# Decayed cumulative sum behind a matmul: four of 32 groups by seven block products, in an order laid out by a planner

## The chip, the cores and the metric

The kernel runs on one core of a Trainium2 chip. The metric is the device time in microseconds of one execution. Engines: PE (matmuls; PEld is its weight load), DVE (vector), ACT (scalar), POOL (GpSimd), SP (here it only issues stores). Every engine works through its own instruction list in order; waits on other engines are semaphores written into the program when it is built.

## What is computed

```python
# x (16, 2048, 1024), w (1024, 1024), decay (1024), all float32
xw = x @ w
out[:, 0, :] = xw[:, 0, :]
for t in range(1, S):
    out[:, t, :] = decay[None, :] * out[:, t - 1, :] + xw[:, t, :]
```

A matmul of 32,768 rows by 1024 x 1024, then a first-order recurrence along time for each batch and column.

## The kernel before

**Tiling.** Time is cut into chunks of 512 (`TL`), four to a batch, 64 in all; two chunks make a group (`groups`), 32 groups. The last group runs as two single chunks. The 1024 output columns are eight blocks of 128 (`n`). One step is one group times one column block: 264 steps, `slots`. A step's result lies with its 128 columns on the partitions and its 1024 times along the free dimension, as the recurrence wants it.

**A chunk's way in.** `load` (L105) brings a quarter of a chunk by a DMA issued from POOL, float32 in memory to bf16 on the chip, 256 KB as landed (four such per chunk, ring `xb` of three). `turn` (L115) transposes it in 32 x 32 blocks on DVE into `xw`; `part` (L123) has ACT copy it, in two halves ("X", "Y"), into `xt` (ring of five), the form that PE reads.

**A step.** `matmul` (L131): eight slices k of the inner dimension times two chunks, 16 matmuls of 128 x 128 by 512 columns, into `ps`, two PSUM banks; there are three such tiles. Then the recurrence, in one of two ways:

- *full* (`run`, L228; every fourth step): DVE scans all 1024 times out of PSUM into `so`, one instruction.
- *paired* (three of four steps): ACT copies the result to `xs` (L185) and writes the decayed even times to `h` (L170); POOL adds them to the odd times (L205); DVE scans the odd times alone with the squared decay (L210), 512 elements; ACT decays the scanned odd times (L170 again), and POOL adds the even ones (L253, "fill").

`save` (L257) and `zero` (L201, L199) carry the last value from one group of a batch to the next. `back` (L265) has DVE transpose `so` in 32 x 32 blocks into `ot`. Four steps fill one `ot` tile, here called a lump, 2 MB; when its fourth back transpose is recorded, `Outlet.store` (L289) issues four DMAs of 512 KB from SP. `ot` is a ring of four, `so` of four, `xs` of three, `h` of four.

**Order.** Everything is pinned to the order in which the Python program records it. The first 34 steps and the last 20 follow `agenda`, a table written by hand (P: paired beginning, S: scan, C: even times, B: back, T: turn, X/Y: chunk copies, L: a load; small letters are single instructions). The steps between follow `usual` with `later`: step s issues the paired beginning of s, the scan of s-1, the fill of s-1, the back transposes of s-2, and one load, with a chunk's turn and copies a fixed number of steps ahead. Line 395 on is the ending, where PE transposes the last tiles and ACT and DVE copy them out (L399).

Of the kernel before, what the change touches and what calls it, by code (L numbers as in the profile page):

```python
# [2 lines left out]

# [6 lines left out]
FP32 = mybir.dt.float32  # L10
# [15 lines left out]
def kernel(  # L26
# [26 lines left out]
    nc = tc.nc  # L53
# [12 lines left out]
    R = K // 2  # L66
    CH = D // 2
    CR = CH // NQ

    const = ctx.enter_context(tc.tile_pool(name="const", bufs=1))  # L70
    sb = ctx.enter_context(tc.tile_pool(name="sb", bufs=1))
# [20 lines left out]
    wcols = wsb.rearrange("p k (h r) q i -> p k h q r i", h=2)  # L92

    def ot_tile(nj):
        return ring(sb, "ot", 4, [128, nj, CR])

    xb_of = {}
    xw_of = {}
# [19 lines left out]

    def part(c, copy, m0, m1, j0=0, j1=NJ):
        if c not in xt_of:  # L120
            xt_of[c] = ring(sb, "xt", 5, [128, M, 2, TL], BF16)
        src = xw_of[c][:, m0:m1, j0:j1].rearrange("p m j i e -> p m e (j i)")
        pin(copy(out=xt_of[c][:, m0:m1, :, j0 * P:j1 * P], in_=src))  # L123

# [16 lines left out]
    class Tile:  # L141
# [3 lines left out]
        def __init__(self, g, n, ps, outlets):  # L145
            self.b, self.t0 = chunks[g[0]]
            self.T = TL * len(g)
            self.n, self.ps, self.outlets = n, ps, outlets
            self.paired = n % R != R - 1
            if len(tiles) in flips or len(tiles) - len(slots) in flips:  # L150
                self.paired = not self.paired
            self.turn = len(tiles)
            self.lot = sum(t.paired for t in tiles)
            self.prev = None if self.t0 == 0 else last[n]
            if self.t0 + self.T < S:
                last[n] = const.tile([128, 1], FP32, name=f"keep{n}", bufs=2)
                self.keep = last[n]
            else:
                self.keep = None

        @property
        def so(self):
            if not hasattr(self, "held"):
                self.held = sb.tile([128, 2 * TL + 2], FP32, name=f"so{self.turn % 4}")
            return self.held

        def decayed(self, src, h=None):
            if h is None:
                h = ring(sb, "h", 4, [128, TL])[:, 0:self.T // 2]
            pin(nc.scalar.activation(  # L170
                out=h, in_=src, func=mybir.ActivationFunctionType.Copy,
                scale=dec[:, self.n:self.n + 1]))
            return h
# [5 lines left out]
                self.zero()  # L179
                self.join()  # L180

        def copy(self):
            self.xs = sb.tile([128, 2 * TL], FP32, name=f"xs{self.lot % 3}")[:, 0:self.T]
            for t, ps in self.parts():
                pin(nc.scalar.copy(out=self.xs[:, t:t + ps.shape[1]], in_=ps))  # L185

        def odd(self):
            self.g = ring(sb, "h", 4, [128, TL])[:, 0:self.T // 2]
            for t, ps in self.parts():
                size = ps.shape[1]  # L190
                self.decayed(ps[:, 0:size:2], self.g[:, t // 2:(t + size) // 2])

        def parts(self):
            some = self.ps if isinstance(self.ps, tuple) else (self.ps,)
            return [(i * self.T // len(some), ps) for i, ps in enumerate(some)]

        def zero(self):
            if self.prev is None:
                pin(nc.gpsimd.memset(self.so[:, 1:2], 0.0))  # L199
            else:  # L200
                pin(nc.scalar.copy(out=self.so[:, 1:2], in_=self.prev))  # L201

        def join(self):
            odds = self.xs[:, 1:self.T:2]
            pin(nc.gpsimd.tensor_tensor(out=odds, in0=self.g, in1=odds, op=ALU.add))  # L205

        def scan(self):
            T, n, so = self.T, self.n, self.so
            if self.paired:
                pin(nc.vector.tensor_tensor_scan(  # L210
                    out=so[:, 3:T + 2:2],
                    data0=squares[-1][:, n:n + 1].to_broadcast([128, T // 2]),
                    data1=self.xs[:, 1:T:2],
                    initial=0.0 if self.prev is None else self.prev,
                    op0=ALU.mult,
                    op1=ALU.add,
                ))
            else:
                for t, ps in self.parts():
                    self.run(ps, t, ps.shape[1])  # L220

        def run(self, ps, t, size):
            n, so = self.n, self.so
            if t:
                before = so[:, t + 1:t + 2]
            else:
                before = 0.0 if self.prev is None else self.prev
            pin(nc.vector.tensor_tensor_scan(  # L228
                out=so[:, t + 2:t + 2 + size],
                data0=dec[:, n:n + 1].to_broadcast([128, size]),  # L230
                data1=ps,
                initial=before,
                op0=ALU.mult,
                op1=ALU.add,
            ))
# [5 lines left out]
        def complete(self):  # L241
            if self.paired:
                self.even()
                self.fill()
            if self.keep is not None:
                self.save()

        def even(self):
            self.h = self.decayed(self.so[:, 1:self.T + 1:2])

        def fill(self):
            T = self.T
            pin(nc.gpsimd.tensor_tensor(  # L253
                out=self.so[:, 2:T + 2:2], in0=self.h, in1=self.xs[:, 0:T:2], op=ALU.add))

        def save(self):
            pin(nc.scalar.copy(out=self.keep, in_=self.so[:, self.T + 1:self.T + 2]))  # L257

        def back(self, half=None):
# [13 lines left out]
    class Outlet:  # L273


        def __init__(self, ns, nj, half=0, queues=(nc.sync,), pieces=1):
            self.pieces = pieces
            self.ns, self.missing, self.half = ns, set(ns), half
            self.nj, self.t0, self.queues = nj, half * nj * P, queues
            self.ot = ot_tile(nj)  # L280

        def store(self, b, t0):
            n0 = self.ns[0]
# [132 lines left out]
    def turn_and_load(c):  # L416
# [58 lines left out]
        18: "g16 T7 L h15 j16 p17 g17 B14 z17 c15 X7",  # L475
        19: "S16 j17 p18 B15 L g18 L S17 k16 h16 z18 j18",
        20: "Y7 S19 L c16 k17 h17 T8 k19 L c17",
        21: "p20 g20 L S18 X8 j20 B17 B19",
        22: "L h18 p21 c18 B16 k18 g21 B18 Y8 z20 L j21 S20",
        23: "p22 z21 z22 S21 L h20 g22 T9 c20 h21",  # L480
        24: "k21 k20 j22 S23 X9 L c21 Y9 B20 L",
        25: "B23 k23 p24 B21 g24 z24 j24 S22 z25",
        26: "p25 T10 k22 h22 g25 c22 S24 X10 j25",
        27: "B22 p26 S25 g26 z26 Y10 j26",
        28: "S27 h25 h24 c25 S26 c24",
        29: "B27 h26 c26 T11 p28 g28 j28 B24",
        30: "p29 B25 g29 z28 j29 S28 z29 S29",
        31: "h28 p30 c28 B26 g30 h29 B28 j30 z30",
        32: "c29 S31 S30 h30 B29 c30 p32 g32 z32 j32 B30 B31 L L",
        33: "p33 g33 z33 j33 S32 h32 c32 k32 L L",  # L490
        -20: "z-20",
        -19: "p-20 g-20",
        -18: "j-20 S-19 S-20 k-19 B-19",
# [16 lines left out]
        -1: "S-2 h-4 c-4 a-1 b-1 V",  # L510
    }
    flips = (1, 13, 15, -19, -18, -11, -8, -6, -3, -2)
    later = {}
    begun = {"T": 12, "X": 11, "Y": 11}
    for c in range(5, nch):
        first = c // 2 * K
        ahead = (7, 6, 4) if c % 2 else (11, 10, 8)
        for letter, a in zip("TXY", ahead):
            if c >= begun[letter]:
                later.setdefault(first - a, []).append(f"{letter}{c}")  # L520

    def usual(s):
        paired = [t.paired for t in tiles]
        do = [f"P{s}"] if paired[s] else []
        if paired[s - 1]:
            do.append(f"S{s - 1}")
        if not paired[s]:
            do.append(f"S{s}")
        do.append(f"C{s - 1}")
        if paired[s - 2]:  # L530
            do.append(f"B{s - 2}")
        if not paired[s - 1]:
            do.append(f"B{s - 1}")
        return do + later.get(s, []) + ["L"] * (2 if len(loads) > NQ else 1)

    def rest(s):
        do = [f"S{s - 1}"] if tiles[s - 1].paired else []
        do.append(f"C{s - 1}")
        if tiles[s - 2].paired:
            do.append(f"B{s - 2}")  # L540
        return do + [f"B{s - 1}"] + later.get(s, []) + ["L"] * len(loads)

    def perform(do):
        for deed in do:
            deeds[deed[0]](int(deed[1:] or 0))

    perform(agenda[-99].split())
    spares = [spare] + [ring(psp, "spare1", 1, [128, TL])]
    for step, (g, n) in enumerate(slots):
        T = TL * len(g)  # L550
        left = step - len(slots)
        if n % R == 0:
            ns, nj = range(n, n + R), T // P
            outlets = [Outlet(ns, nj)]
        if left == -R:
            outlets = []
        if step == 0:
# [48 lines left out]
            for k, l in todo:  # L606
                matmul(ps[:, l * TL:(l + 1) * TL], n, k, xt_of[g[l]])
        tiles.append(Tile(g, n, ps, outlets))
        do = agenda.get(step, agenda.get(left) if left >= -20 else None)
        if do is None:  # L610
            do = usual(step)
        else:
            do = do.split()
            if left == -20:
                do = rest(step) + do
        perform(do)
    assert not loads
# [1 line left out]
_INS = ['x', 'w', 'decay']  # L619
# [26 lines left out]
```

## Time and profile before

| | |
|---|---|
| median of 3 runs | 904.89 us (904.84 to 904.93) |
| the profiled execution, its own time | 905.68 us |
| its span | 903.9 us |
| granted TensorE clock, mean | 0.999 |
| matmuls, weight loads | 4217, 4217 |
| DMA | 204.77 MB moved, mean 227 GB/s |
| HBM read, written | 138.42 MB, 134.22 MB |

One execution is profiled. Busy time is the time in which an engine works on an instruction; an instruction's duration overlaps the start of the next by some 0.1 us, so the distance from start to start says more of what a full engine can do. A stretch is a piece of the span, in us from its start. "L131" is a line of the kernel above.

### The profile page before, as it was taken

Reading aid. Unit: us, or ns where it says so; the run is one execution under the profiler, and the core shown is the slowest. Engines: PE = TensorE matmul, PEld = TensorE weight load, DVE = VectorE, ACT = ScalarE, POOL = GpSimd, SP = SyncE. Lnnn points to the kernel's source line nnn. Section 1 sums busy time; section 2 is a strip of 40 time slices with the busy share of each in tenths; the row PEclk is TensorE's granted clock in tenths of the full one; section 3 lists DMA queues with packets and bytes.
Section 4 is the critical chain, followed back from the end, with each engine's and each line's share of the span. In section 5 each row is a group of like instructions: output and inputs, shape, how many; then the busy total and the mean of one; then the engine's idle time right before and its main releaser. Section 6 shows DMA issues by size and latency. Waiting matters only on the chain.

```text
span 903.9 us, 12113 instructions
## 1 busy us (share of the span) xinstructions
PE 896.4 (99%) x4217; PEld 412.7 (46%) x4217; DVE 825.5 (91%) x628; ACT 686.3 (76%) x957; POOL 656.7 (73%) x755
## 2 busy tenths in 40 slices
PE   8999999999999999999999999999999999999997
PEld 5544444444444444444444444444444444444444
DVE  4999998999999999999998999999999999999997
ACT  4899967777877877877778778778777787787742
POOL 7978678777767768677677677777777776776632
PEclk9999999999999999999999999999999999999999
DMA  9999999999999999999999999999999999999868
GB/s 186 190 215 215 226 256 217 215 237 236 254 242 260 243 251 257 248 237 226 224 237 229 224 229 229 230 224 229 231 227 228 233 232 222 226 233 211 176 143 235
DMA packets 402542, 204.77 MB, mean 227 GB/s; under 512 B 8752, under 2 KB 401456, under 8 KB 402480
## 3 DMA queue, kind: packets, MB, share of 16 engines
q1 hardware_dynamic: 265168, 134.76, 61.0%
q0 software_dynamic: 137024, 68.70, 56.6%
q8 instruction: 33, 0.54, 0.2%
q10 hardware_dynamic: 288, 0.52, 0.2%
q14 instruction: 29, 0.24, 0.1%
HBM read 138.42 MB, written 134.22 MB: 302 GB/s over the span
## 4 chain that ended last, share of the span: by engine, by line
PE 97%; DMA 1%; POOL 0%; issue 0%; DVE 0%; DVEq 0%; POOLq 0%
PE ps L131 96%; DMA xb<-in_x_dram 1%; PE spare L131 1%; POOL xb L105 0%; PE spare L395 0%; PE ps L395 0%; DVE h L399 0%; DVE xw L115 0%; DVEq L115 0%; POOLq L630 0%
## 5 line engine op out<-in xcount | busy, mean ns | idle before, releaser
L131 PE MATMUL ps<-xt,wsb 128*128 128x512 bf16 (+1 forms) x4028 | 866.3, 378 | 0.0
L131 PEld LDWEIGHTS <-wsb 128*128 128x128 bf16 x4168 | 407.5, 98 | 478.0 <-ACT wsb L313 0.8
L205 POOL TENSOR_TENSOR xs<-h,xs 128x512 f32<-128x512 f32 (+1 forms) x190 | 242.8, 1278 | 188.1 <-ACT h L170 85.3
L185 ACT COPY xs<-ps 128x1024 f32<-128x1024 f32 (+1 forms) x190 | 188.9, 994 | 152.9 <-PE ps L131 148.1
L265 DVE STREAM_TRANSPOSE ot<-so 128x1024 f32<-128x1024 f32 (+1 forms) x260 | 300.0, 1191 | 2.1 <-POOL so L199 1.1
L253 POOL TENSOR_TENSOR so<-h,xs 128x512 f32<-128x512 f32 (+1 forms) x190 | 241.0, 1270 | 43.7 <-ACT h L170 27.8
L123 ACT COPY xt<-xw 128x2048 bf16<-128x2048 bf16 (+3 forms) x136 | 242.3, 1790 | 8.7 <-DVE xw L115 8.7
L105 POOL DMA_DIRECT2D xb<-in_x_dram x264 | 174.0, 660 | 5.6 <-DMA xb<-in_x_dram 3.2
L170 ACT ACTIVATE h<-so,dec 128x512 f32<-128x512 f32 (+1 forms) x190 | 145.3, 766 | 28.7 <-DVE so L210 25.2
L115 DVE STREAM_TRANSPOSE xw<-xb 128x2048 f32<-128x2048 f32 (+3 forms) x78 | 147.4, 1901 | 8.0 <-DMA xb<-in_x_dram 7.9
L210 DVE TENSOR_TENSOR_SCAN so<-spare,keep,xs 128x512 f32<-128x512 f32 (+1 forms) x97 | 119.9, 1239 | 26.7 <-POOL xs L205 26.4
L210 DVE TENSOR_TENSOR_SCAN so<-spare,xs 128x512 f32<-128x512 f32 x93 | 113.3, 1219 | 27.4 <-POOL xs L205 24.5
L170 ACT ACTIVATE h<-ps,dec 128x512 f32<-128x512 f32 (+1 forms) x190 | 130.0, 684 | 0.0
L228 DVE TENSOR_TENSOR_SCAN so<-dec,ps 128x1024 f32<-128x1024 f32 x34 | 76.8, 2260 | 1.0 <-ACT h L170 1.0
L228 DVE TENSOR_TENSOR_SCAN so<-dec,keep,ps 128x1024 f32<-128x1024 f32 (+1 forms) x35 | 75.9, 2168 | 0.2 <-issue 0.2
L257 ACT COPY keep<-so 128x1 f32<-128x1 f32 x136 | 25.3, 188 | 9.5 <-DVE so L228 9.0
L201 ACT COPY so<-keep 128x1 f32<-128x1 f32 x97 | 18.4, 191 | 2.7 <-DVE ot L265 2.4
L131 PE MATMUL spare<-xt,wsb 128*128 128x512 bf16 (+3 forms) x60 | 12.6, 329 | 0.0
L131 PE MATMUL ps<-xw,wsb 128*128 128x256 bf16 (+3 forms) x68 | 11.2, 301 | 0.4 <-DVE xw L115 0.4
L199 POOL MEMSET so<- 128x1 f32 x93 | 10.7, 117 | 0.6 <-DVE ot L265 0.6
L331 PE MATMUL spare<-idle 128*128 128x512 bf16 x22 | 6.8, 479 | 1.2 <-DVE idle L321 1.2
L306 POOL DMA_DIRECT2D ot<-in_w_dram x12 | 6.6, 552 | 1.7 <-DMA xb<-in_x_dram 0.8
(39 smaller groups left out, 37.9 us busy)
## 6 DMA issues: line engine op xcount, KB each, us to landing
out_dram<-ot SPq DMA_DIRECT2D x248, 512.0 KB, 10.9
xb<-in_x_dram POOLq DMA_DIRECT2D x248, 256.0 KB, 7.9
out_dram<-ot SPq DMA_DIRECT2D x12, 256.0 KB, 4.2
ot<-in_w_dram POOLq DMA_DIRECT2D x12, 128.0 KB, 5.6
xb<-in_x_dram POOLq DMA_DIRECT2D x8, 128.0 KB, 5.4
out_dram<-xb SPq DMA_DIRECT2D x3, 256.0 KB
xb<-in_x_dram POOLq DMA_DIRECT2D x4, 144.0 KB, 7.0
ot<-in_w_dram ACTq DMA_DIRECT2D x2, 256.0 KB, 5.2
```

The lines of the kernel that those rows point to most:

```text
L105: pin(nc.gpsimd.dma_start(out=xb_of[c][quad(q), j0:j1], in_=_ap(x, [[D, P], [P * D, j1 - j0], [1, CQ]], (b * S + t0 + j0 * P) * D + q * CQ)))
L115: pin(nc.vector.transpose(out=dst.rearrange("p (m j i) -> p j m i", m=M, i=P)[:, j0:j1, m0:m1], in_=src.rearrange("p (j m c) -> p j m c", ...
L123: pin(copy(out=xt_of[c][:, m0:m1, :, j0 * P:j1 * P], in_=src))
L131: pin(nc.tensor.matmul(out=ps[:, t0:t1] if ps.shape[1] >= t1 else ps, lhsT=lhs, rhs=rhs, start=(k == 0 and t0 == start), stop=(stop and k ...
L170: pin(nc.scalar.activation(out=h, in_=src, func=mybir.ActivationFunctionType.Copy, scale=dec[:, self.n:self.n + 1]))
L185: pin(nc.scalar.copy(out=self.xs[:, t:t + ps.shape[1]], in_=ps))
L205: pin(nc.gpsimd.tensor_tensor(out=odds, in0=self.g, in1=odds, op=ALU.add))
L210: pin(nc.vector.tensor_tensor_scan(out=so[:, 3:T + 2:2], data0=squares[-1][:, n:n + 1].to_broadcast([128, T // 2]), data1=self.xs[:, 1:T:2 ...
L228: pin(nc.vector.tensor_tensor_scan(out=so[:, t + 2:t + 2 + size], data0=dec[:, n:n + 1].to_broadcast([128, size]), data1=ps, initial=befor ...
L253: pin(nc.gpsimd.tensor_tensor(out=self.so[:, 2:T + 2:2], in0=self.h, in1=self.xs[:, 0:T:2], op=ALU.add))
L257: pin(nc.scalar.copy(out=self.keep, in_=self.so[:, self.T + 1:self.T + 2]))
L265: pin(nc.vector.transpose(out=outlet.ot[:, :, c0:c0 + P], in_=self.so[:, 2 + t0:2 + t0 + nj * P].rearrange("p (i t) -> p i t", t=P)))
```

## The change

A *merged* group is worked out by seven products of blocks instead of eight. The group's 1024 input columns are cut in two halves of 512 (k below and above 4) and the chunks and column blocks in pairs: two chunks a, b times two column blocks n0, n1, each a sum over two halves, are eight products of four matmuls. Sums of the inputs (`sums`, three on DVE, one on POOL, once a group) and differences of the weights (`differ`, on POOL, 20 in all, made once ahead of the first merged group, kept in `wd`) allow seven. Their results are put together through PSUM: a product is accumulated, copied out by ACT (`lift`), further products are accumulated on top, copied or joined again (`join`, DVE, an addition or subtraction of a PSUM operand and an SBUF one, 512 elements). For two column blocks: four copies and three joins. Steps of merged groups are all paired and take their recurrence from `so`, since no whole result stands in PSUM.

Groups 10, 15, 20 and 25 are merged. In the groups around them fewer steps are full: of groups 4 to 30 (steps 34 to 243) 36 steps are, by `SHARE`.

Steps 34 to 243 are no longer recorded by `usual` but by `steady`: every instruction becomes a `Job` with an engine, a cost, a key (a due time) and what it comes after; `in_order` lays them out, engine by engine, always the ready job with the lowest key, and records them in that order. Rings change: `ot` 3 (was 4), `xt` 4 (was 5), `so` 7 (was 4), `xs` is gone (the paired steps work in place in `so`). A turn is recorded in two halves. Loads get evenly spaced due times, at least 2.8 apart, 50 ahead of their group (74 ahead of a merged one). A lump is stored by sixteen DMAs of 128 KB, everywhere. The hand-written steps 21 to 33 move X8 to X10 and drop the last loads, which the planner takes over.

```diff
+    OTS, XTS, SOS, HS = 3, 4, 7, 4
+    FROM, TO = 34, 244
+    SUMS, SUMT = ('dve', 'dve', 'dve', 'pool'), -16
+    WBY, WLEAD, WSTEP = "pool", 130, 6
+    SHARE = {-1: 0.25, 0: 0, 1: 0.08, 2: 0.16, 3: 0.25, 9: 0.25}
+    merged = (10, 15, 20, 25)
...
-        return ring(sb, "ot", 4, [128, nj, CR])
+        return ring(sb, "ot", OTS, [128, nj, CR])
...
-        def __init__(self, ns, nj, half=0, queues=(nc.sync,), pieces=1):
+        def __init__(self, ns, nj, half=0, queues=(nc.sync,), pieces=4):
...
-        24: "k21 k20 j22 S23 X9 L c21 Y9 B20 L",
+        24: "X8 k21 k20 j22 S23 Y8 L c21 B20 L",
...
-        32: "c29 S31 S30 h30 B29 c30 p32 g32 z32 j32 B30 B31 L L",
-        33: "p33 g33 z33 j33 S32 h32 c32 k32 L L",
+        32: "c29 X10 Y10 S31 S30 h30 B29 c30 p32 g32 z32 j32 B30 B31",
+        33: "p33 g33 z33 j33",
...
+    GAP = 0.19
+    BEGUN = {"pe": 0.0, "act": 7.6, "dve": 8.3, "pool": 9.0}
+    LAND = 11.0
+    STORED = 13.0
+    PASS = 0.2158
+    cost = {"p": .91, "g": .6, "z": .12, "j": 1.27, "S": 1.16, "D": 2.2, "h": .68, "c": 1.27,
+            "k": .11, "B": 1.14, "T": 1.14, "X": 1.79, "L": .66, "half": .5, "both": .62,
+            "sum": 2.15, "wpool": 1.15, "wdve": 1.2, "slow": 4.2}
+    each = R * PASS
+    TURN = (0, 3, 4, 5, 6, 8, 9)
+    AHEAD, SPACE = 50, 2.8
+    EXTRA = 24
+    differences = ((1, 0, 1, 1), (1, 1, 0, 0), (0, 0, 0, 1), (0, 1, 1, 1), (1, 0, 0, 0))
+    def differ(d, j):
...
+        pin(by.tensor_tensor(out=wd[:, d, j], in0=one, in1=two, op=ALU.subtract))
...
+        def back(tile, end, key):
...
+            b = Job("dve", cost["B"], key + 6, tile.back,
+                    [end, place.get((s, "k"))] + stored.get(lump - OTS, []) + ([first] if first else []))
...
+            def sums(i, engine):
...
+                out, one, two = ((S1, b[:, 0:2], b[:, 2:4]), (S2, a[:, 0:2], S1),
+                                 (S0, a[:, 2:4], S2), (b[:, 0:2], a[:, 0:2], b[:, 0:2]))[i]
...
+                pin(engine.tensor_tensor(out=flat(out), in0=flat(one), in1=flat(two), op=ALU.add))
...
+            what = {
+                "a1": ("a", lambda: S(0), w_at(0, n0), True, TURN[0]),
+                "a2": ("a", lambda: S(1), w_less(1), False, TURN[1]),
+                "b1": ("b", lambda: S(2), w_at(1, n1), True, TURN[2]),
+                "c": ("c", lambda: xb_()[:, 2:4], w_less(4), True, TURN[3]),
+                "a3": ("a", lambda: xa()[:, 0:2], w_less(2), False, TURN[4]),
+                "b2": ("b", lambda: xa()[:, 2:4], w_less(0), False, TURN[5]),
+                "a4": ("a", lambda: xb_()[:, 0:2], w_less(3), False, TURN[6]),
+            }
...
+            def lift(i, k, where, key, after):
+                return Job("act", cost["half"], key, lambda: pin(nc.scalar.copy(
+                    out=half(i, k), in_=spot(where))), after)
+            def join(i, k, where, op, key, after, turned=False):
+                def do():
+                    one, other = half(i, k), spot(where)
+                    pin(nc.vector.tensor_tensor(
+                        out=half(i, k), in0=other if turned else one,
+                        in1=one if turned else other, op=op))
...
+            a1 = mult("a1", done + weights + (after_ps[bank - 3] if bank >= 3 else []))
+            A1 = lift(0, 1, "a", at("a1"), [a1, gone[0]])
+            a2 = mult("a2", [A1])
+            A2 = lift(0, 0, "a", at("a2"), [a2, gone[0]])
+            b1 = mult("b1", [a1])
+            B1 = lift(1, 0, "b", at("b1"), [b1, gone[1]])
+            c = mult("c", [after_spare[0], part_of[c1, 1]])
+            C = join(0, 1, "c", ALU.add, at("c"), [c, A1])
+            after_spare[0] = C
+            a3 = mult("a3", [A2])
+            A3 = join(1, 0, "a", ALU.subtract, at("a3"), [a3, B1])
+            b2 = mult("b2", [B1])
+            B2 = join(0, 0, "b", ALU.subtract, at("b2"), [b2, A2], True)
+            a4 = mult("a4", [A3])
+            A4 = lift(1, 1, "a", at("a4"), [a4, gone[1]])
+            after_ps[bank] += [B2, A4]
```

In the changed kernel lines have moved: L781 holds the sums, L623 the weight differences, L840 the copies of the products, L846 the joins, L138 and L764 the matmuls.

## The prediction

> **What bounds the kernel now.** I read the page first: engine shares, then the chain that ended last.
>
> ```profile
> PE 896.4 (99%) x4217; PEld 412.7 (46%) x4217; DVE 825.5 (91%) x628; ACT 686.3 (76%) x957; POOL 656.7 (73%) x755
> ...
> PE 97%; DMA 1%; POOL 0%; issue 0%; DVE 0%; DVEq 0%; POOLq 0%
> ```
>
> PE holds 97% of the chain and waits for another engine only 2.3 us in all (in its view of waits), all of it in the start. So only fewer matmuls, or a shorter head or tail, can shorten this kernel. DVE is next with 91%. To see whether that is spare room or a second limit I took the table of stretches, then DVE in order of time where it is fullest (50 to 100 us: 49.92 busy).
>
> ```profile
> 282.80:310.40 27.60, 27.60 (x129) 12.52 (x128) 25.57 (x19) 21.45 (x29) 20.78 (x25) 1.00 1.24 251
> ...
> 60.51 1.20 DVE L265 STREAM_TRANSPOSE ot<-so 128x1024 f32<-128x1024 f32 x1
> 61.63 1.25 DVE L210 TENSOR_TENSOR_SCAN so<-spare,keep,xs 128x512 f32<-128x512 f32 x1
> 62.80 2.34 DVE L265 STREAM_TRANSPOSE ot<-so 128x1024 f32<-128x1024 f32 x2
> 65.06 2.31 DVE L228 TENSOR_TENSOR_SCAN so<-dec,keep,ps 128x1024 f32<-128x1024 f32 x1
> 67.29 1.25 DVE L210 TENSOR_TENSOR_SCAN so<-spare,keep,xs 128x512 f32<-128x512 f32 x1
> 68.46 2.28 DVE L115 STREAM_TRANSPOSE xw<-xb 128x2048 f32<-128x2048 f32 x1
> 70.67 2.33 DVE L265 STREAM_TRANSPOSE ot<-so 128x1024 f32<-128x1024 f32 x2
> ```
>
> The first row is one group: PE, PEld, DVE, ACT, POOL busy, clock, DMA share, GB/s. DVE has 2.0 us left of 27.6, ACT 6.2, POOL 6.8. In the rest, the distance from start to start is what an instruction costs when nothing is awaited: back transpose 1.13, half scan 1.17, full scan 2.23 (2.18 elsewhere; I take 2.20), turn 2.21. A saturated DVE loses almost nothing between them.
>
> Last the stores, which feed back through the ring of lumps. DMA queues in 138.0 to 165.6 us and 331.2 to 358.8 us:
>
> ```profile
> q0 software_dynamic: 5899, 2.93, 76.9%
> q1 hardware_dynamic: 6056, 3.05, 52.7%
> ```
> ```profile
> q1 hardware_dynamic: 9524, 4.80, 64.9%
> q0 software_dynamic: 4281, 2.13, 59.3%
> ```
> ```profile
> 173.64 4.67 SPq L289 DMA_DIRECT2D out_dram<-ot  x1
> ```
>
> q0 is loads, q1 stores, MB per 27.6 us. A group makes 4.19 MB of output. Stores manage 4.80 beside 2.13 of loads, 3.05 beside 2.93. The last row, from SP in order of time, is the first store of the lump whose last back transpose ended at 158.4: 15 us late; by the packets of its queue that lump was out at 198, 40 us after it was filled. By 420 us a store starts as its lump is full.
>
> **The change, part by part.** All sums are against the profiled execution: 905.68 us, that is 1.78 around its span of 903.9, and 0.79 above the median 904.89.
>
> **PE.** Four groups make 112 matmuls of 512 columns where they made 128: 64 fewer. One costs 13.81/64 = 0.2158 us (the full scans of two successive lumps start at 303.54 and 317.35, 64 matmuls apart). 64 x 0.2158 = **-13.81**. Weight loads (98 ns) still lie inside. In the built order PE's other work is unchanged. A merged group takes 24.17 instead of 27.62.
>
> **DVE.** From the merged group's start to the next one's (five groups) the built order has 40 back transposes, 34 half scans, 6 full scans, 20 half turns, 12 joins and 3 sums. Half turns have the size of a back transpose: 1.13. A join (128x512 f32, one operand in PSUM) has two neighbours: the ending's DVE copy out of PSUM at 0.692, the full scan's 512-wide form at 1.255; the cast of 512 elements at 0.424 is the floor. It is nearest to the copy; started back to back like the rows above it loses 0.07: 0.62. A sum (128x2048 bf16, two SBUF operands) lies between four 512-element bf16 copies, 4 x 0.352 = 1.41, and one element a cycle as the turn of 2048 goes, 2.29; I take 2.2. Then 45.2 + 39.8 + 13.2 + 22.6 + 7.4 + 6.6 = **134.8 us** for DVE, where PE needs 24.17 + 4 x 27.62 = 134.65. Fewer full scans (6 where there were 10) already pay for part. So DVE goes from 92% to full: it fits with nothing to spare. Ends: cheapest 134.8 - 12 x 0.20 - 3 x 0.8 = 130; dearest 134.8 + 12 x 0.64 + 3 x 0.1 = 142.8, which is 8.1 over PE four times, 32 us. I cost the middle at 0, hidden only as long as the late work is back transposes (ring of seven result tiles, some 24 us deep).
>
> The Trainium skill (SBUF — State Buffer, section "Who interferes with whom") says that such an instruction and a GpSimd one that reads SBUF exclude one another for a whole instruction; it (VectorE: DVE Perf Modes, section "The perf-mode tier table") gives 1.224 us for a bf16 tensor_tensor of 2048. No row here shows either: the half scan takes its factor from PSUM. By the pages a sum is an estimated 1.22 alone and 1.22 + 1.29 = 2.5 behind a POOL addition; the cycle would be 131.9 or 135.7, and the sign of the forecast would not turn.
>
> **Hand-overs inside a pair.** The products of a pair run into one PSUM bank with copies between (a1, copy, a2, copy, a3, join, a4). In the built order pair 0 of group 10 goes a1, b1, c, a2, the next pair's a1, a3. With units of 4 x 0.2158 = 0.863, a2 ends at 3.45 us, the unit between at 4.32; on ACT a chunk copy (1.85) and the b1 copy (0.50, L185's 512 form less overlap) lie in front of a2's copy, which ends near 4.45, so a3 starts some 0.3 late. DVE's join for a4 lies behind another join and a scan: b2 ends at 6.4, join 0.62, scan 1.17, join 0.62 give 9.0, PE is there at 8.97: 0.2 late. I take 0.35 for each of 16 pairs: **+5.6**; ends 0 and 16 x 1.17 (one scan in front each time) = 18.7.
>
> **Stores and the ring of three.** 260 store issues become 1040, of 128 KB; an issue took 0.32 us where its queue was free (the one at 419.73), 16 x 0.32 = 5.1 of the 24.17/2 = 12.1 us of a merged lump, and SP has nothing else: 0. Each waits on one of eight semaphores, so eight (1 MB) are out at a time; stores need 152 GB/s, 6.9 us for 1 MB, about the landing of today's: 0, and at worst SP's wait joins the next item. The ring of lumps shrinks from four to three. In this trace the lump that is full at 158.4 has landed at 198.2, and the third one after it begins to fill at 189.8: with three buffers DVE would have stood 8.4 us there, the longest such case; from 400 us on there are 17 to spare. Even loads at 2.8 us a piece are 2.58 MB per 27.6 us; between the two rows above that lets 3.8 MB of stores through, 0.4 short, 2.6 us of lag per group; starting from the 22 us of lag at 125 us this comes up to the limit near 230 us, and the pauses ahead of merged groups drain it (6.61 MB of stores beside 0.43 of loads, 110 to 138 us). When the first back transpose of a lump waits, scans, joins and turns stand behind it on DVE, and PE waits for those. I take **+2**; ends 0 and 8.4 plus 4 later times 2 = 16.4.
>
> **ACT, POOL, head.** Merged group on ACT: 16 lifts x 0.50, 16 scalings at 0.58 and 0.66, 8 small x 0.16, X 4 x 1.85: 26.6 of 24.17; the group behind has 6 to spare. POOL: 16 additions x 1.25, 8 load issues x 0.66, one sum at 4 x 1.25 = 5.0: 30.3 of 24.17; the next takes 22.8 of 27.6, so it is level two groups later; fills come late, which the ring of seven covers. The 20 weight differences (1.25, as L205) are 25 us over 120 ahead of group 10, where POOL idles 25%. X8 to X10 come two to eight steps later, with four chunk buffers, and still lead their group. Cover lost, any of these delays joins or scans by an instruction (1.3 us) each time. 0.
>
> Sum: 905.68 - 13.81 + 5.6 + 2 = 899.5, less 0.79: **898.7 us**.
>
> **Rivals.** *Full yield*: copies and joins land in time, no store waits: 905.68 - 13.81 - 0.79 = 891.1. For it: PE waited for nothing in 880 us of before. Against: chain of a2, copy, a3 with two units between. 16%.
>
> *DVE becomes the bound* (slower): place, groups 10 to 29; DVE has no slack and any wait of its own is passed on to PE. Price: now it idles 2.0 of 27.6, mostly for POOL's additions (26.4 and 24.5 us before the half scans). If half of that remains, 3.8%, a cycle is 139.8, 5.1 over PE; four give 20.5, in place of hand-overs: 905.68 - 13.81 + 20.5 - 0.79 = 911.6. It decides slower from 138.1 us a cycle. For: the waits are there today with an easier order. Against: where DVE is backlogged (50 to 100 us) its waits vanish. 27%.
>
> *Stores bind* through the ring of three: 898.7 - 2 + 8.4 = 905.1, no change. For: 40 us of lag at 160 to 210 us; against: lag falls to 15 with even loads. 13%.
>
> That the change is not what it says is ruled out by the built order: 64 matmuls fewer.
>
> **How the numbers follow.** Forecast 42% (895 to 903), full yield 16%, DVE bound 27%, stores 13%, 2% elsewhere (faster). Faster by over 0.2% (about what a measurement of this kernel tells from none; below 903.1): 0.41 + 0.16 + 0.03 + 0.02 = 0.62 with 3 of the 13 for stores. Within: 0.01 + 0.06 + 0.03 = 0.10. Slower: 0.24 + 0.04 = 0.28. The likeliest case's own range is 894 to 903; to leave out two in ten it runs from 892 to 911.
>
> **What would show it.** PE with 4153 matmuls and 13.8 us less busy; its waits near 8 us, half each on ACT L840 and DVE L846, in four blocks. DVE above 97% from 280 to 830 us; DVE sums near 2.2, joins near 0.65. A DVE wait for out_dram near 200 to 250 us of 2 to 4. SP with lag under 30. It is wrong if PE waits in the plain groups as well, or if DVE shows idle time between 280 and 830 us while PE waits for it.

## The result, and the profile after

| | before | after |
|---|---|---|
| median of 4 runs, us | 904.91 (904.84 to 904.98) | 925.88 (925.72 to 927.16) |
| ratio, 95% interval | | 1.0235 (1.0217 to 1.0253) |
| span of the profiled execution | 903.9 | 925.3 |
| matmul weight loads | 4217 | 4153 |

Slower by 2.3%, and outside the range of 892 to 911. The page of after answers to the two lines first shown of before, engine shares and the chain by engine:

```profile
PE 885.6 (96%) x4073; PEld 406.7 (44%) x4153; DVE 842.4 (91%) x740; ACT 721.5 (78%) x1047; POOL 745.0 (81%) x822
...
PE 43%; DMA 28%; DVE 12%; issue 5%; SPq 5%; ACT 4%; POOL 1%; DVEq 0%; another core or an unknown queue 0%; ACTq 0%; POOLq 0%
```

The profiled execution of after is the longest of its four (927.16). The weight loads show that the 64 matmuls are gone (80 matmul records are missing from this trace). But PE's 97% of the chain has become 43%; 28% belongs to DMAs. To see where the time went I noted when PE begins each group (its first weight load) and subtracted before's times. Worked out from the two traces, in us; the other columns are experiments explained below:

| PE begins | before | after | e5 | e9 | e13 |
|---|---|---|---|---|---|
| group 10 | 288.6 | +0.9 | -0.2 | +0.1 | -0.0 |
| group 26 | 730.6 | -1.3 | -2.2 | -1.9 | -4.5 |
| group 28 | 785.9 | +7.7 | -1.3 | -1.0 | -2.9 |
| group 30 | 841.1 | +10.0 | +7.1 | -1.0 | +5.4 |
| end of the matmuls | 898.5 | +11.5 | +7.2 | -0.9 | +6.1 |
| end of the span | 903.9 | +21.4 | +7.3 | +0.2 | +5.9 |

So after's +21.4 has four parts: +0.9 ahead of group 10; -2.2 over the stretch with the merged groups, where 13.8 were to be saved, so that 11.6 were lost there; +12.8 from group 26 to the last matmul; +9.9 behind the last matmul.

*The late wait.* After's waits (total, times, longest), the rows of DVE for stores and of PE:

```profile
DVE ot L276 <- DMA out_dram<-ot: 26.0, 9, 11.7
PE ps L138 <- ACT h L184: 7.8, 5, 6.0
PE ps L764 <- ACT so L840: 7.5, 10, 1.1
PE ps L764 <- DVE so L846: 0.9, 2, 0.6
```

The longest, in order of time (start, duration, engine, line; in brackets the idle time and what ended it), first DVE, then PE:

```profile
766.82 1.20 DVE L221 TENSOR_TENSOR_SCAN so<-spare,so 128x512 f32<-128x512 f32 x1
779.75 2.37 DVE L276 STREAM_TRANSPOSE ot<-so 128x1024 f32<-128x1024 f32 x2 [11.74 <-DMA out_dram<-ot]
```
```profile
771.68 7.07 PE L138 MATMUL ps<-xt,wsb 128*128 128x512 bf16 x31
784.75 5.13 PE L138 MATMUL ps<-xt,wsb 128*128 128x512 bf16 x16 [6.00 <-ACT h L184]
```

DVE stands from 768.0 to 779.8 before the first back transpose of a lump, because the lump three before it is not out yet. Scans queue behind it, ACT's even times behind those, and PE's wait is put down to ACT, the last link. PE loses 6.2 us (from start to start, as all losses here), then runs seven matmuls at half speed.

*The end.* SP in order of time, after and then before; `xb` and `h` are the last tiles:

```profile
886.92 33.04 SPq L305 DMA_DIRECT2D out_dram<-ot  x64
920.06 1.37 SPq L417 DMA_DIRECT2D out_dram<-xb  x3
```
```profile
878.17 18.29 SPq L289 DMA_DIRECT2D out_dram<-ot  x13
898.18 1.63 SPq L401 DMA_DIRECT2D out_dram<-xb  x3
```

Before had issued its last lump at 896.5, ahead of the last tiles. After issues 64 transfers without a pause until 920.0, 0.52 us each, and the last tiles stand behind them. Not all are of 128 KB: the last three lumps are of half the size, so the last 48 transfers are of 64 KB.

### The profile page after: what moved, and what is told of

It reads as the page before. It is cut to its first block, busy times and chain, and to the rows that moved or that the text cites. A ratio compares the mean times of both kernels' runs of the same rounds, so it can differ in the third digit from the quotient of the medians.

```text
span 925.3 us, 12918 instructions
## 1 busy us (share of the span) xinstructions
PE 885.6 (96%) x4073; PEld 406.7 (44%) x4153; DVE 842.4 (91%) x740; ACT 721.5 (78%) x1047; POOL 745.0 (81%) x822
## 4 chain that ended last, share of the span: by engine, by line
PE 43%; DMA 28%; DVE 12%; issue 5%; SPq 5%; ACT 4%; POOL 1%; DVEq 0%; another core or an unknown queue 0%; ACTq 0%; POOLq 0%
PE ps L138 39%; DMA out_dram<-ot 26%; SPq L305 5%; DVE ot L276 4%; DVE so L221 3%; PE ps L764 3%; DVE xw L122 2%; DMA xb<-in_x_dram 2%; DVE so L239 2%; ACT xt L130 1%; ACT h L184 1%; ACT so L840 1%; DMA ot<-in_w_dram 1%; DVE sx L781 0%; PE spare L138 0%
## 5 line engine op out<-in xcount | busy, mean ns | idle before, releaser
L138 PE MATMUL ps<-xt,wsb 128*128 128x512 bf16 (+1 forms) x3447 | 757.2, 378 | 13.3 <-ACT h L184 7.8
L138 PEld LDWEIGHTS <-wsb 128*128 128x128 bf16 x3656 | 357.7, 98 | 430.5 <-issue 15.4
L264 POOL TENSOR_TENSOR so<-h,so 128x512 f32<-128x512 f32 (+1 forms) x207 | 267.1, 1298 | 111.2 <-ACT h L184 72.8
L216 POOL TENSOR_TENSOR so<-h,so 128x512 f32<-128x512 f32 (+1 forms) x207 | 269.9, 1307 | 42.4 <-ACT h L184 26.6
L184 ACT ACTIVATE h<-so,dec 128x512 f32<-128x512 f32 (+1 forms) x240 | 182.7, 771 | 71.6 <-DVE so L221 67.0
L202 ACT COPY so<-ps 128x1024 f32<-128x1024 f32 (+1 forms) x175 | 174.2, 995 | 61.2 <-PE ps L138 59.3
L122 DVE STREAM_TRANSPOSE xw<-xb 128x1024 f32<-128x1024 f32 (+4 forms) x130 | 152.9, 1192 | 6.4 <-DMA xb<-in_x_dram 6.3
L221 DVE TENSOR_TENSOR_SCAN so<-spare,keep,so 128x512 f32<-128x512 f32 (+1 forms) x105 | 126.0, 1214 | 0.0
L221 DVE TENSOR_TENSOR_SCAN so<-spare,so 128x512 f32<-128x512 f32 x102 | 120.6, 1193 | 4.6 <-POOL so L216 3.7
L764 PE MATMUL ps<-xt,wd 128*128 128x512 bf16 x187 | 46.7, 378 | 7.7 <-ACT so L840 6.5
L764 PEld LDWEIGHTS <-wd 128*128 128x128 bf16 x320 | 31.1, 97 | 48.9 <-issue 13.1
L840 ACT COPY so<-ps 128x512 f32<-128x512 f32 x64 | 36.1, 592 | 11.1 <-PE ps L764 6.4
L764 PE MATMUL ps<-sx,wsb 128*128 128x512 bf16 x127 | 31.8, 379 | 1.2 <-ACT so L840 1.0
L623 POOL TENSOR_TENSOR wd<-wsb 128x512 bf16<-128x512 bf16 x20 | 23.3, 1163 | 0.1
L846 DVE TENSOR_TENSOR so<-ps,so 128x512 f32<-128x512 f32 x16 | 11.0, 687 | 12.1 <-PE ps L764 10.2
```

What stands on the lines that cost most here:

```text
L122: pin(nc.vector.transpose(out=dst.rearrange("p (m j i) -> p j m i", m=M, i=P)[:, j0:j1, m0:m1], in_=src.rearrange("p (j m c) -> p j m c", ...
L138: pin(nc.tensor.matmul(out=ps[:, t0:t1] if ps.shape[1] >= t1 else ps, lhsT=lhs, rhs=rhs, start=(k == 0 and t0 == start), stop=(stop and k ...
L184: pin(nc.scalar.activation(out=h, in_=src, func=mybir.ActivationFunctionType.Copy, scale=dec[:, self.n:self.n + 1]))
L202: pin(nc.scalar.copy(out=self.line[:, t:t + ps.shape[1]], in_=ps))
L221: pin(nc.vector.tensor_tensor_scan(out=so[:, 3:T + 2:2], data0=squares[-1][:, n:n + 1].to_broadcast([128, T // 2]), data1=so[:, 3:T + 2:2] ...
L264: pin(nc.gpsimd.tensor_tensor(out=evens, in0=self.h, in1=evens, op=ALU.add))
```

## The experiments

Ratios are to the kernel before, measured beside each (905.16 to 905.26).

**e1: one transfer a quarter again** (four a lump).

```diff
-        def __init__(self, ns, nj, half=0, queues=(nc.sync,), pieces=4):
+        def __init__(self, ns, nj, half=0, queues=(nc.sync,), pieces=1):
```

> The changed kernel with lumps stored in four transfers again (1 piece, not 4). Theory A (sixteen transfers, of which only eight are out at a time, make the stores slow; late stores hold DVE through the ring of three, and the end waits for them): DVE's wait for out_dram falls from 26.0 us to under 4, the time from the last matmul to the end from 15.2 us to about 5.5, PE loses nothing between 758 and 794 us beyond 1; total 925.9 - 9.9 - 9 - 2 = 905, within 3. Rival B (the ring of three alone is to blame): the end recovers, DVE still waits 15 us or more for out_dram; total about 915. Rival C (neither): 925.

915.98 us, ratio 1.0105 (1.0075 to 1.0136). From the last matmul to the end: 5.5 us, as before the change, where after has 15.3. DVE's waits for stores do not go: 21.6 us in eleven, with PE losses at 215, 709 and 829 us, in the profiled execution, which is the longest of six (908.59 to 920.70). The median is what rival B gave. So the end is the transfers' doing, and the waits are not.

**e2: the kernel before with sixteen transfers a lump** (the same edit the other way round).

> The kernel before with nothing changed but lumps stored in sixteen transfers; its ring of lumps stays at four. Theory A: the stores fall behind in the steady part too (a lump takes 13 to 14 us of SP, SP hardly idles), no PE stall since four lumps cover it, the end is 8 to 11 us longer: about 914. Rival (the split costs nothing, the long end comes from the plan): 905.

914.52 us, ratio 1.0103 (1.0083 to 1.0124). PE ends 0.4 us earlier than in before, and the span is 9.0 longer. SP at the end:

```profile
879.98 27.57 SPq L289 DMA_DIRECT2D out_dram<-ot  x53
907.65 1.37 SPq L401 DMA_DIRECT2D out_dram<-xb  x3
```

The same picture without planner or merged groups: sixteen transfers cost 9.4 us, all of it at the end. With four lumps DVE waits for stores only 1.4 us.

**e3: the plan alone** (`merged = ()`, all else as in after).

> The changed kernel with no merged group: the planner, the rings, the paced loads and the sixteen transfers alone; all matmuls are back. Theory A: no hand-overs, hence none of the 12 us that PE lost in merged groups, nor the 13.8 saved; the end stays 10 us long; with loads at 3.45 us apart the lag stays under 30 us and DVE waits less than 10 us for out_dram: 915 to 920. Rival (the planned order itself costs the time): over 925. Rival (the merged groups alone cost it): 905.

916.9 us, ratio 1.013 (1.011 to 1.015). PE is 0.5 to 1.0 later than before all the way, the end takes 15.5. DVE waits for stores 9.2 us in four, without a loss on PE. Planner and rings cost about 1 us here; the merged groups bring both other losses, the hand-overs and the late wait.

**e4: sixteen transfers, but four for the last lumps; e5: also, the planner's clock runs on.** In after the planner's time stops at step 244, so the loads of the last groups get due times crowded together.

```diff
-        return [Outlet(range(n, n + R), len(g) * NJ)]
+        return [Outlet(range(n, n + R), len(g) * NJ, pieces=4 if step < TO else 1)]
...
-            if s < TO:
-                t += (7 if c // 2 in merged else 8) * 2 * PASS
+            t += (7 if c // 2 in merged else 8) * len(slots[s][0]) * PASS
```

> The changed kernel with four transfers a lump from step 244 on only, sixteen before. Theory A: the end is 5 to 7 us from the last matmul, the rest as in the changed kernel: 925.9 - 9 = 917. Rival (the long end comes from the lag that has built up before, not from the last lumps' own transfers): 922 or more.

> As the run with four transfers from step 244 on (917.9 us), and the planner's clock runs on after step 244, so the last chunks' loads get due times 3.45 us apart and no longer push those before them together to 2.8 us. Theory D (where the plan packs loads closer than 3.45 us, stores get under the 4.19 MB that a group makes, lag rises to the ring of three, DVE waits and PE after it): in 700 to 770 us loads fall from 2.1 to 2.4 MB per 27.6 us to 2.1, PE loses under 2 us in groups 27 and 28 instead of 9, total 908 to 910. Rival (the wait comes from the merged groups' faster lumps, loads have no part): 916 to 919, the same wait of 12 us near 768.

e4: 917.9 us, ratio 1.0141 (1.0121 to 1.0161); the end takes 5.3, the wait stays (12.2 us at 767). The lumps before step 244 still go out in sixteen, so the long end comes from the last lumps' own transfers and not from a lag built up before. e5: 913.44 us, ratio 1.0089 (1.0074 to 1.0104); no loss at groups 27 and 28, but a wait of 8.6 at 812 costs PE 5.6 there. Moving the loads moved the wait and did not end it.

**e6: loads spaced evenly everywhere** (e5 with `EXTRA = 0`, no earlier loads for merged groups).

> The same with EXTRA = 0: loads of merged groups no earlier than the others, so no packing to 2.8 us ahead of groups 10, 15, 20 and 25 and no pauses behind. Theory D: store lag under 25 us throughout, DVE waits for out_dram under 5 us in all (22.0 with four transfers at the end only), total 906 to 909; the merged groups' own loss stays near 12 us. Rival (merged groups need their loads early): PE waits for chunk copies at the start of merged groups, 912 or more.

918.94 us, ratio 1.0148 (1.0122 to 1.0174). PE starts group 26 9.0 us late. The store waits stay at 20.5, which speaks against theory D. The rival's time came, but its cause is not shown: the profile puts PE's waits at the beginning of merged groups (up to 2.6 us) down to ACT's copies out of PSUM and its even times, not to chunk copies.

**e7: the planner told that a store takes 28 us, not 13** (e4 with `STORED = 28.0`).

> As the run with four transfers from step 244 on (917.9 us), but the planner takes a lump to be stored 28 us after its last back transpose, as the trace has it (20 to 30), instead of 13. Nothing changes in the transfers. Theory E (DVE stands idle because the plan puts a back transpose where its buffer is not yet out, with ready work behind it): DVE waits for out_dram fall from 22 us to under 5 and PE's loss in groups 27 and 28 from 9 to under 3: 908 to 911. Rival (the stores are too slow whatever the order): DVE has nothing else to do, PE waits for result tiles, 915 to 919.

915.08 us, ratio 1.0096 (1.0073 to 1.0118). The longest wait falls to 5.3, but there are seven, 17.2 in all, PE loses 4.2 at 838, and the merged groups lose more (in the profiled execution, the longest of 911.89 to 916.51). Neither expectation is met cleanly.

**e8: chunk copies in quarters** (e5; ACT's 1.9 us copies cut into two of 1.05).

```diff
-                    part_of[c, half] = Job(
-                        "act", cost["X"], need + 3 + 3 * half,
-                        lambda c=c, h=half: part(c, nc.scalar.copy, h * M // 2, (h + 1) * M // 2),
+                    one = Job(
+                        "act", .95, need + 3 + 3 * half,
+                        lambda c=c, h=half: part(c, nc.scalar.copy, 2 * h, 2 * h + 1),
...
+                    part_of[c, half] = Job(
+                        "act", .95, need + 3.01 + 3 * half,
+                        lambda c=c, h=half: part(c, nc.scalar.copy, 2 * h + 1, 2 * h + 2), [one])
```

> As the run with the planner's clock running on, and each chunk is copied on ACT in quarters of about 0.95 us instead of halves of 1.85. Theory F (part of the 12 us lost in merged groups is a2's copy standing behind a chunk copy on ACT): PE's first loss in a merged group, 1.02 to 1.05 us behind a2, goes to under 0.3, the four groups together lose 8 to 9 us instead of 12, total 3 us under the run with the clock alone. Rival (hand-overs lose to DVE's joins): no difference.

911.28 us, ratio 1.0067 (1.005 to 1.0084). The first loss in a merged group is 0.84 to 0.89, where under 0.3 was expected. The four merged groups lose 7.9 us in place of e5's 11.1, so the long copy has a part in it; but the plain groups between them lose 3.7 in place of 0.8, and from group 10 to 26 it is about 11.5 against 11.8. The new order lays one bare hand-over open, on PE:

```profile
292.91 1.03 PE L766 MATMUL ps<-sx,wd 128*128 128x512 bf16 x4
294.67 1.02 PE L766 MATMUL ps<-xt,wd 128*128 128x512 bf16 x4 [0.73 <-ACT so L842]
```

and on ACT:

```profile
294.03 1.07 ACT L842 COPY so<-ps 128x512 f32<-128x512 f32 x2 [0.25 <-PE ps L766]
```

A product begun at 292.91 takes 0.86 at the pace of the others, to 293.77. The copy that waits for its end starts 0.26 later, on an ACT that stood idle, and the product that waits for this copy follows at 294.67: 0.90 us from product over copy to product with nothing in front, one whole unit of 0.863. By the program as built, though, the product begun at 292.91 is a2, the copy is that of b1, which had ended at 292.05, and the product behind it is b2. Why b1's copy waits for a2 is told with the hand-overs below.

**e9: a quarter of the output not stored in steps 36 to 243** (e5).

> As the run with the planner's clock running on (913.4 us), but lumps of the planned steps are stored in three of their four parts (a quarter of the output of steps 36 to 243 is left out). The order of all engines' instructions stays. Theory D (what is lost outside the merged groups is bandwidth: the stores of a lump are not out when the ring of three comes round): DVE waits for out_dram fall from 20 us to under 3, PE loses nothing after group 26, the merged groups lose the same 11.8 of 13.8 as before: 904 to 905. Rival G (the order waits for something else and the DMA is only named): 911 or more.

905.19 us, ratio 0.9999 (0.999 to 1.0009). After group 26 PE loses only 1.0 us; the hand-over loss stays 11.8 or so (from +0.1 to -1.9, of 13.8). DVE still waits 6.1 us for stores, in two (at 98 and 139 us; under 3 was expected), without a loss on PE. So e5's late waits, and the 8.2 us by which it is slower than e9, are lack of store bandwidth against three lumps.

**e10: light back transposes in the merged groups** (e5; one of 32 blocks, and their lumps not stored).

> As the run with the planner's clock running on, but in merged groups the back transpose moves one block of 32 instead of 32 blocks, and these groups' lumps are not stored (the output of groups 10, 15, 20 and 25 is left out). 8 x about 1.0 us is taken from DVE in each, order unchanged. Theory H (the merged groups lose because DVE has more work than 24 us holds and joins stand behind it): PE's loss in the four groups falls from 11.8 us to under 5. Rival I (they lose to the chain product, copy, product and to the order of ACT): 9 us or more.

909.39 us, ratio 1.0044 (1.0028 to 1.006). With DVE relieved, PE's losses inside the merged groups repeat e9's to 0.03 us (1.02, 0.41, 0.90, 1.26, 0.75 in group 10 and just behind), but for one: 0.94 at 730.7, behind a join, is gone. Its waits:

```profile
PE ps L765 <- ACT so L841: 7.1, 10, 1.1
PE ps L765 <- DVE so L847: 0.9, 2, 0.6
```

But for that one, DVE's load in merged groups is not what PE waits for. The run is slower than e9 by what PE loses behind a wait for stores of 4.9 us at 811.

**e11: the kernel before with three lumps** (`ring(sb, "ot", 3, ...)`).

> The kernel before with its ring of lumps at three instead of four, nothing else. By its own trace lumps 2 to 4 and 7 to 14 land up to 8.5 us after the buffer would be wanted. Theory D: DVE waits for out_dram between 95 and 260 us, some 9 to 12 us in all, and PE loses 3 to 8 us there: 908 to 913. Rival (a ring of three costs nothing at this rate): 905.

914.09 us, ratio 1.0102 (1.0086 to 1.0119). DVE's longest wait:

```profile
185.67 1.25 DVE L265 STREAM_TRANSPOSE ot<-so 128x1024 f32<-128x1024 f32 x1 [6.83 <-DMA out_dram<-ot]
```

PE loses 4.8 and then 2.5 on twelve slow matmuls. DVE's two other waits for stores are 3.15 and 1.40. So a ring of three costs the old kernel, too, something of this size, at 185 us.

**e12: one merged group** (e5 with `merged = (25,)`).

> As the run with the planner's clock running on, with group 25 alone merged. It saves 3.45 us and in that run lost 1.25 of them there. With one group the stores keep the pace of four groups before it: if waits for out_dram come from the pace and the earlier loads of merged groups, DVE waits under 8 us in all, PE loses nothing else: 903 to 904, under the kernel before. Rival (group 25's early loads and the end's bunching bring the wait of 8 us near 812 again): 909 to 911.

912.75 us, ratio 1.0084 (1.0069 to 1.0099). Both expected times are missed. The group keeps 0.7 of its 3.45 us when PE begins group 26; then 6.6 are lost by the end: 1.1 ahead of the group's last product (a join), 1.0 at 826, 2.1 at 849, 1.5 at 876 to 878 and smaller ones. The store waits are 10.3 in five, of which 4.4 stand at 99 us and cost nothing. That the late losses come from the others (2.5 at 801, 2.8 at 818) is not shown.

**e13: another order of the seven products** (e5; more products between a copy and the product on top of it). **e14: e13 without a quarter of the stores of steps 36 to 243. e15: e13 with groups 10 and 15 alone.**

```diff
-    TURN = (0, 3, 4, 5, 6, 8, 9)
+    TURN = (0, 4, 2, 3, 8, 6, 12)
...
-    merged = (10, 15, 20, 25)
+    merged = (10, 15)
```

> As the run with the planner's clock running on (913.4 us), with the due times of a pair's seven products spread, TURN = (0, 4, 2, 3, 8, 6, 12): three units of other products between a product and the one that needs its copy, where there were two. Theory I (the merged groups lose 11.8 of their 13.8 us because a copy on ACT, standing behind other ACT work, ends later than PE has other products for): the four groups lose 7 or less. Total 909 to 911 if the wait for stores near 812 stays. Rival (the planner fills PE by what is ready, so due times change little): 11 to 12 lost again, 913.

> The same with a quarter of the output of steps 36 to 243 not stored, to read the merged groups without the stores. Theory I: 905.2 less what the spread wins in merged groups, 900 to 902. Rival: 905.

> As the first of these, with groups 10 and 15 alone merged, a complete kernel. If the spread works and no merged group stands near the end, 905.3 - 6.9 + 3 + 0.5 = 902 us, under the kernel before; if waits for stores come all the same, 906 to 910.

e13: 911.82 us, ratio 1.0076 (1.0059 to 1.0093). The merged groups keep 4.5 of 13.8: a loss of 9.3 in place of e5's 11.8, short of the 7 expected. PE's waits by engine are now 4.7 for ACT's copies and 2.0 for the joins; from start to start its fourteen losses behind them come to 9.2, which is nearly all (copies 6.4, joins 2.8). e14: 903.42 us, ratio 0.998 (0.9971 to 0.9989), with part of the output left out; 900 to 902 was expected. e15: 908.85 us, ratio 1.0047 (1.0032 to 1.0062): 1.0 ahead of before until group 30, then one stop of PE with slow matmuls behind costs 4.2. The rival's time came, but no wait for a store stands just ahead (the last is 1.65 at 811); ACT has two chunk copies in front of the work that PE waits for. No version that stores all of the output beats the kernel before.

## Why the prediction was wrong, step by step

| term | predicted | measured | shown by |
|---|---|---|---|
| 64 matmuls fewer | -13.81 | -13.8 | weight loads 4153 |
| DVE full | 0 | near 0 | e10 |
| hand-overs | +5.6 | +11.6 | positions; e13 moves it |
| ring of three, stores, plan | +2 | +0.9 and +12.8 | e9, e11, e3 |
| sixteen transfers | 0 | +9.9 | e1, e2, e4 |
| span | -6.2 | +21.4 | |

**Sixteen transfers at 0: the step that failed outright.** I took an issue at 0.32 from a moment when SP's queue was free, summed sixteen of them against a merged lump, and reasoned that eight transfers out, now 1 MB, suffice at the mean rate. That does no harm on the way: e2 loses nothing before the last matmul. I never summed the issues at the end, although I summed against the span's end, and there SP itself is the limit. In after the first issue behind a stop takes 0.32 us; each one right behind another takes 0.52, from start to start. The 64 issues from 886.9 on make 33.1 us. At 0.32 they would have been done by 907.4, ahead of the last matmul (910.0), and would have cost nothing. After's waits of SP over the whole span, then those from 886.5 to 920.0, and the last 48 transfers (size, median us from issue to landing):

```profile
SPq L305 <- DMA out_dram<-ot: 316.9, 399, 1.9
```
```profile
SPq L305 <- DVE ot L276: 4.0, 1, 4.0
```
```profile
out_dram<-ot SPq DMA_DIRECT2D x48, 64.0 KB, 1.8
```

On the way SP waits for an earlier store ahead of many issues. At the end it does not: its one wait there comes before the first of the 64, and a transfer lands 1.8 us after its issue, well before its semaphore is wanted again 4.2 us later. So it is neither a backlog from before (e4) nor the limit of eight out, but the number of issues. In before SP's largest entry was 293.5 us for the back transposes, for work to hand on. Why an issue behind another takes 0.52 us the runs don't show.

**The ring of three at +2: right mechanism, wrong place and size.** e11 bears out the reading of before's lag: I had reckoned 8.4 us of wait for the longest case with three lumps, DVE waited 6.83, and PE lost 7.3 with the slow matmuls behind. The rival of the stores was this, at 13%. What failed is "from 400 us on there are 17 to spare": this was the lag of the old load order, carried over to a new one. In after the loads come bunched. After's DMA queues (packets, MB, share) from 745.3 to 772.9 us, and then from 772.9 to 800.5:

```profile
q0 software_dynamic: 4757, 2.37, 65.3%
q1 hardware_dynamic: 7292, 3.52, 55.1%
```
```profile
q1 hardware_dynamic: 8600, 4.15, 61.3%
q0 software_dynamic: 2249, 1.12, 32.4%
```

The first has 3.52 MB of stores, where a group makes 4.19. That is also less than the 3.8 that I read off before's two rows for 2.58 MB of loads. SP's lag was 20 to 30 us from a full lump to its landing, as I had said ("under 30"), but three lumps of 13.8 us bear no more than that. The waits that I had put near 200 to 250 us came (1.8, 0.4 and 1.6 us at 205 to 234) and cost PE nothing; the costly one came at 768 us, in a plain group, as the sign of being wrong had it. e5 and e7 move it, e9 ends it. e3 has ring and planner without the wait's cost, so the merged groups have a part in it; whether by their shorter lumps or by their earlier loads stays open.

**Hand-overs at +5.6: right mechanism, half the size, one wait overlooked.** I followed pair 0 of group 10 and put the copy of a2 at 4.45 us after its a1 began and a3 0.3 late. In after, PE (products of four matmuls; the first row holds two) and ACT:

```profile
289.73 1.89 PE L764 MATMUL ps<-sx,wsb 128*128 128x512 bf16 x8
291.45 1.03 PE L764 MATMUL spare<-xt,wd 128*128 128x512 bf16 x4
292.31 1.03 PE L764 MATMUL ps<-sx,wd 128*128 128x512 bf16 x4
293.18 1.03 PE L764 MATMUL ps<-sx,wsb 128*128 128x512 bf16 x4
295.06 1.89 PE L764 MATMUL ps<-xt,wd 128*128 128x512 bf16 x8 [0.86 <-ACT so L840]
```
```profile
291.65 0.59 ACT L840 COPY so<-ps 128x512 f32<-128x512 f32 x1 [0.71 <-PE ps L764]
292.14 1.90 ACT L130 COPY xt<-xw 128x2048 bf16<-128x2048 bf16 x1
293.94 1.08 ACT L840 COPY so<-ps 128x512 f32<-128x512 f32 x2
```

PE's side is as reckoned so far: a2 ends at 293.18, 3.45 after 289.73, and one unit follows. But ACT's first copy starts at 291.65, only when b1 has ended too, though ACT had idled 0.71: the chunk copy and the next two copies move back by that. a2's copy ends at 295.02, 5.29 after a1 began, and the next product is 1.02 late. Of the 0.84 beyond the 4.45 reckoned, 0.71 is that wait.

Its cause stands in the program as built: a copy waits for the last write to its whole tile `ps`, both banks, and not to its own half. Of the eight matmuls from 289.73 (a1 and b1) only the eighth signals, so a1's copy waits for b1; b1's copy waits for a2. The two copies at 293.94 are b1's and then a2's, and only the second signals. The product at 295.06 is b2 and then a3, not a3 first as I had it; b2 needs only b1's copy and starts behind a2's. I had taken the two halves as independent. Tiles of their own for the two halves were not tried, so what they would win back is not shown.

Beyond that I had ACT's queue busy without a gap, counted no signal time, and took 0.35 as the mean of a pair with one wait; group 10 alone has losses of 1.02, 0.41, 0.90 and 1.28. Nor do copies and joins share evenly, 7.5 us to 0.9. By merged group after loses 3.8, 3.7, 2.4 and 1.0 of the 3.45 that each saves (and 0.75 just behind the first), so groups 10 and 15 cost more than they save. The hand-over of e8 (0.90, more than a unit) says that a distance of one unit doesn't hold even with nothing in front of the copy.

**DVE at 0: right, with one price off.** Joins took 0.66 to 0.69 (0.62 taken). From group 10 to group 15 and from there to group 20 DVE was busy 131 and 134 us (134.8 reckoned), 94% and 97%; I had said above 97% throughout. From 600 to 700 us it is busy 99.5 of 100, and PE loses nothing there. The 27% rival of a full DVE came nearest in time, 911.6, by a mechanism that e10 excludes for the merged groups. Of the twelve sums seven cost 1.18 and five 2.20, not 2.2 always. DVE and then POOL ahead of group 10:

```profile
276.26 1.18 DVE L781 TENSOR_TENSOR sx<-xt 128x2048 bf16<-128x2048 bf16 x1
277.48 2.20 DVE L781 TENSOR_TENSOR sx<-xt,sx 128x2048 bf16<-128x2048 bf16 x1
```
```profile
276.69 1.92 POOL L264 TENSOR_TENSOR so<-h,so 128x512 f32<-128x512 f32 x1 [1.85 <-ACT h L184]
278.57 4.53 POOL L216 TENSOR_TENSOR so<-h,so 128x512 f32<-128x512 f32 x2
```

The first sum runs alone and ends at 277.44; POOL's addition, issued at 276.69, ends 1.17 after that. The second sum, issued at 277.48, ends 1.07 after POOL's (278.61). Each takes its turn as a whole: the addition's 1.92 and 2.26 were 1.30 without a sum beside it. Here the trace agrees with the Trainium skill (SBUF — State Buffer, "Who interferes with whom"), by which a DVE instruction with two SBUF inputs and a GpSimd one that reads SBUF exclude one another; I had put its 1.22 and 2.5 aside for lack of a row.

**ACT, POOL and head at 0**: e3 bears out plan, rings and head to within 1 us. It has no merged group, so it says nothing of ACT's and POOL's load in those; no run here parts that from the hand-overs. **Full yield** needed hand-overs in time, and in no merged group were they all.

## What to carry to other kernels

Splitting a transfer is free only while the issuing engine has time for it: count the issues of the last lumps at the pace of one behind another (here 0.52 us), since the last result stands behind them in the same queue. A saving on PE that turns one accumulation into a chain through another engine is worth its matmuls less the hand-overs, here 0.72 us a pair of the 0.86 saved; count from the end of the product to the start of the next with every instruction in front of the copy, and read in the program as built what the copy waits for. And a ring that loses a buffer has to be judged by the lag in the new order, not by the lag that the old order left.

## What the hardware showed beside

After a stop PE runs at half speed for a while: seven matmuls at 0.43 us behind 6.2 us (after), twelve behind 4.8 (e11), but also eight behind 2.2 (e15) and 2.4 (e1), and none behind 2.1 (e12) or 2.3 (e7). The Trainium skill (TensorE: Matmul & The Clock Gate, "Part 1: The HAM clock gate") puts the drop behind an idle window of about 3.4 us at no fixed phase. The eight slow ones, 3.4 us, fit its length, and so do the trace's records of the clock, which show half speed for 3.41 us (e15, 857.28 to 860.70) or twice that (after, 781.02 to 787.85); stops of 2.2 us bring it on here too, so not every drop needs a whole such window of idle time.

Not tried: a ring of four lumps beside the merged groups' buffers.
